# An early 64 KB store of zeros on the ScalarE DMA queue of a streaming p = 2 pooling kernel

## The chip, the cores and the metric

The kernel runs on one core of a Trainium2 chip. The metric is device time in microseconds of that core. Three runs of the kernel before gave 393.93, 393.96 and 393.99 us; the median is 393.96 us.

## What is computed

The input x is 32 x 256 x 4096 float32, the output 32 x 256 x 1024 float32. Each output is the root of the mean of the squares of four neighbours:

```python
for i in range(out_length):                   # out_length = 4096 // 4
    window = np.abs(x[:, :, 4*i:4*i+4]) ** p  # p = 2
    result[:, :, i] = np.mean(window, axis=-1) ** (1.0 / p)
```

The core reads 134.22 MB and writes 33.55 MB; nothing is read twice.

## The kernel before

Input and output are taken as flat arrays and cut into 20 pieces, numbered 0 to 19. A piece is 128 partitions by W = 13184 elements (52,736 bytes in each partition); piece 3 and the last one are a little narrower. Neighbouring pieces form six blocks (line 51), and within a block each partition holds one contiguous row of the flat array, so that a store of a block writes long rows.

Each piece goes through the same steps: a load by SyncE's queue (`load`, line 83); a square in place on ScalarE (`square`, line 89); two adds on VectorE that fold four squares into one sum (`pairs`, line 95, and `fours`, line 99); a square root with scale 1/4 on ScalarE (`roots`, line 102); and one store for each block (`store`, line 86). There are three input buffers `xt`, so load i + 3 is issued by SyncE after the adds of piece i. The results of a block gather in `ot`, four pieces wide. The sums of pieces 4, 8, 12 and 16 wait in `st`, in PSUM.

The order on each engine is written out by hand (`manual_schedule`, line 62): the three first loads at lines 122 and 123; a tiny square root at line 129, which brings in ScalarE's function table; the loop over pieces 0 to 16 from line 130; and a hand-written tail for pieces 17 to 19. The stores of blocks 0, 1 and 2 are issued by ScalarE on its own DMA queue (line 116, after the last roots of the block); the stores of blocks 3, 4 and 5 are issued by SyncE, on the queue that carries the loads. In the profile SyncE's queue is q1 and ScalarE's is q10. A DMA of 128 rows is seen in the trace as 128 packets, one for each row, eight on each of the 16 DMA engines, and 16 packets of 4 bytes that signal the end.

ScalarE's queue is used for the first time by the store of block 0.

Of the kernel before, what the change touches and what calls it, by code (L numbers as in the profile page):

```python
# [1 line left out]

# [4 lines left out]


@with_exitstack
def kernel(  # L10
    ctx: ExitStack,
    tc: tile.TileContext,
    x: bass.AP,
    p: float,
    kernel_size: int,
    out: bass.AP,
):

    nc = tc.nc

    assert float(p) == 2.0, "kernel specialized for p == 2"
    k = int(kernel_size)  # L30
    assert k == 4, "kernel specialized for kernel_size == 4"

    P = nc.NUM_PARTITIONS
    fp32 = mybir.dt.float32
    Act = mybir.ActivationFunctionType
    add = mybir.AluOpType.add
    xf = x.rearrange("b c l -> (b c l)")
    of = out.rearrange("b c l -> (b c l)")
    total = xf.shape[0] // P

    W = 13184
    R = W // k
    X_SLOTS = 3
    NARROW = W - 32
    LAST = total - 18 * W - NARROW
    widths = [W] * 3 + [NARROW] + [W] * 15 + [LAST]
    n = len(widths)
    assert 0 < LAST <= W and LAST % 16 == 0


    blocks = [[0, 1, 2, 3], [4, 5, 6, 7], [8, 9, 10, 11], [12, 13, 14, 15], [18, 16, 17], [19]]
    block_of = {i: b for b, group in enumerate(blocks) for i in group}
    block_width = [sum(widths[i] for i in group) for group in blocks]

    x_pool = ctx.enter_context(tc.tile_pool(name="x_pool", bufs=1))
    o_pool = ctx.enter_context(tc.tile_pool(name="o_pool", bufs=1))
    s_pool = ctx.enter_context(tc.tile_pool(name="s_pool", bufs=1, space=bass.MemoryType.PSUM))
    x_tiles = [x_pool.tile([P, W], fp32, name=f"xt{j}") for j in range(X_SLOTS)]
    o_tile = o_pool.tile([P, 4 * R], fp32, name="ot")
    first = o_pool.tile([P, 1], fp32, name="first")  # L60
    s_tile = s_pool.tile([P, 4096], fp32, name="st")
    ctx.enter_context(tc.manual_schedule())

    def rows(flat, b, div):
        at = sum(block_width[:b]) * P // div
        return flat[at:at + block_width[b] * P // div].rearrange("(p w) -> p w", p=P)


    free = x_tiles[17 % X_SLOTS]
    place = {i: o_tile[:, i % 4 * R:i % 4 * R + widths[i] // k] for i in range(16)}  # L70
    place[18] = free[:, R:2 * R]
    place[19] = free[:, 0:LAST // k]
    place[16] = free[:, 2 * R:3 * R]
    place[17] = free[:, 3 * R:4 * R]
    held = [o_tile[:, 0:w // k] for w in block_width[:4]] + [free[:, R:4 * R], place[19]]

    xs, loads, stores, sums, squares = {}, {}, {}, {}, {}

    def load(i):
        b = block_of[i]  # L80
        at = sum(widths[j] for j in blocks[b][:blocks[b].index(i)])
        xs[i] = x_tiles[i % X_SLOTS][:, 0:widths[i]]
        loads[i] = nc.sync.dma_start(out=xs[i], in_=rows(xf, b, 1)[:, at:at + widths[i]])  # L83

    def store(b, queue):
        stores[b] = queue.dma_start(out=rows(of, b, k), in_=held[b])  # L86

    def square(v):
        return nc.scalar.activation(out=v, in_=v, func=Act.Square)  # L89

    def pairs(v):

        q = v.rearrange("p (n j) -> p n j", j=k)
        h = v[:, 0:v.shape[1] // 2].rearrange("p (n j) -> p n j", j=2)
        return nc.vector.tensor_tensor(out=h, in0=q[:, :, 0:2], in1=q[:, :, 2:4], op=add)  # L95

    def fours(o, v):
        h = v[:, 0:v.shape[1] // 2].rearrange("p (n j) -> p n j", j=2)
        return nc.vector.tensor_tensor(out=o, in0=h[:, :, 0], in1=h[:, :, 1], op=add)  # L99

    def root(o, s):
        return nc.scalar.activation(out=o, in_=s, func=Act.Sqrt, scale=1.0 / k)  # L102

    summed = {i: s_tile[:, 0:R] if i in (4, 8, 12, 16) else place[i] for i in range(n)}

    def roots(*group):
        if len(group) == 1:
            root(place[group[0]], summed[group[0]])
        else:
            v = o_tile[:, group[0] % 4 * R:(group[-1] % 4 + 1) * R]  # L110
            r = root(v, v)
            if group[0] in (5, 9):

                implied(r, stores[block_of[group[0]] - 1])
        if group[-1] in (3, 7, 11):
            store(block_of[group[-1]], nc.scalar)

    def implied(later, earlier):

        tc.declare_no_dep(later.ins, earlier.ins, reason="implied by the other waits")  # L120

    for i in range(X_SLOTS):
        load(i)


    ahead = {4: (3,), 8: (7,), 12: (11,)}
    behind = {3: [(0, 1, 2)], 7: [(5, 6), (4,)], 11: [(9, 10), (8,)], 14: [(12,)], 15: [(13, 14)], 16: [(15,)]}

    root(first[:, :], nc.const_aps.tensor(1.0, (P, 1), fp32))
    for i in range(17):  # L130
        if i in ahead:
            roots(*ahead[i])
        s = square(xs[i])
        squares[i] = s
        if i == 3:
            implied(s, squares[0])
        if i in (3, 7, 11):

            for earlier in sums[i - X_SLOTS]:
                implied(s, earlier)  # L140
        for group in behind.get(i, []):
            roots(*group)
        sums[i] = pairs(xs[i]), fours(summed[i], xs[i])
        if i + X_SLOTS < n:
            load(i + X_SLOTS)

    store(3, nc.sync)
    square(xs[17])
    pairs(xs[17])
    fours(summed[17], xs[17])  # L150
    later = {18: 4608, 19: 2000}

    def shared_square(i):
        v = xs[i][:, 0:later[i]]
        nc.vector.tensor_tensor(out=v, in0=v, in1=v, op=mybir.AluOpType.mult)  # L155
        square(xs[i][:, later[i]:widths[i]])

    def shared_pairs(i):
        implied(pairs(xs[i]), loads[i])

    shared_square(18)
    roots(16)
    roots(17)
    shared_pairs(18)
    fours(summed[18], xs[18])
    shared_square(19)
    roots(18)
    store(4, nc.sync)
    shared_pairs(19)
    fours(summed[19], xs[19])  # L170
    roots(19)
    store(5, nc.sync)


# [1 line left out]
_INS = ['x', 'p', 'kernel_size']  # L176
_OUTS = [((32, 256, 1024), 'float32')]

_NUMBERS = {'p': 2.0, 'kernel_size': 4}


# [26 lines left out]
```

## Time and profile before

| what | value |
|---|---|
| median of three runs | 393.96 us |
| span of the profiled execution, first to last instruction | 392.3 us |
| median less span (what lies outside the span) | 1.7 us |
| ScalarE busy | 274.4 us, 70% |
| VectorE busy | 218.2 us, 56% |
| q1: share of the 16 DMA engines' span, packets | 87.4%, 3312 |
| q10: share of the 16 DMA engines' span, packets | 11.9%, 432 |
| moved over the span | 167.77 MB, 428 GB/s |
| issues by ScalarE's queue | 3, from 90.3 to 247.1 us |

The table gives no separate time for the profiled execution beyond its span: its own time is taken as the span and the 1.7 us around it, which together make the median. Busy times count compute instructions alone; a DMA's work is in the queue rows. In the table of 40 slices one slice is 9.8 us. In a table by stretches, a DMA packet is counted whole in the stretch in which it starts: over a few microseconds the share and the GB/s can be above what the engines can do, or far below it, and it is the product with the stretch's length that means something.

### The profile page before, as it was taken

Reading aid. Unit: us, or ns where it says so; the run is one execution under the profiler, and the core shown is the slowest. Engines: PE = TensorE matmul, PEld = TensorE weight load, DVE = VectorE, ACT = ScalarE, POOL = GpSimd, SP = SyncE. Lnnn points to the kernel's source line nnn. Section 1 sums busy time; section 2 is a strip of 40 time slices with the busy share of each in tenths; the row PEclk is TensorE's granted clock in tenths of the full one; section 3 lists DMA queues with packets and bytes.
Section 4 is the critical chain, followed back from the end, with each engine's and each line's share of the span. In section 5 each row is a group of like instructions: output and inputs, shape, how many; then the busy total and the mean of one; then the engine's idle time right before and its main releaser. Section 6 shows DMA issues by size and latency. Waiting matters only on the chain.

```text
span 392.3 us, 176 instructions
## 1 busy us (share of the span) xinstructions
DVE 218.2 (56%) x42; ACT 274.4 (70%) x37; POOL 0.2 (0%) x4
## 2 busy tenths in 40 slices
DVE  0009477580693274905942748069418485699970
ACT  1095695979950859799509597995098999969910
POOL 0000000000000000000000000000000000000000
DMA  8999999999999999999999999999999999999997
GB/s 344 430 430 430 430 440 435 452 457 366 430 430 430 430 430 430 430 441 446 452 446 441 436 430 436 430 430 430 430 430 430 430 430 430 430 453 415 430 413 342
DMA packets 3744, 167.77 MB, mean 428 GB/s; under 512 B 416, under 2 KB 416, under 8 KB 416
## 3 DMA queue, kind: packets, MB, share of 16 engines
q1 hardware_dynamic: 3312, 147.53, 87.4%
q10 hardware_dynamic: 432, 20.25, 11.9%
HBM read 134.22 MB, written 33.55 MB: 428 GB/s over the span
## 4 chain that ended last, share of the span: by engine, by line
DMA 43%; ACT 30%; DVE 23%; issue 0%; ACTq 0%; SPq 0%; DVEq 0%
DMA xt<-in_x_dram 43%; ACT xt L89 28%; DVE xt L95 14%; DVE ot L99 5%; DVE xt L99 3%; DVE xt L155 2%; ACT ot L102 2%; ACT xt L102 1%; ACTq L86 0%; SPq L83 0%; DVEq L95 0%
## 5 line engine op out<-in xcount | busy, mean ns | idle before, releaser
L89 ACT ACTIVATE xt<-xt 128x13184 f32<-128x13184 f32 (+3 forms) x20 | 216.7, 10847 | 92.3 <-DMA xt<-in_x_dram 91.0
L95 DVE TENSOR_TENSOR xt<-xt 128x6592 f32<-128x6592 f32 (+2 forms) x20 | 139.7, 6985 | 144.1 <-ACT xt L89 143.9
L99 DVE TENSOR_TENSOR ot<-xt 128x3296 f32<-128x3296 f32 (+1 forms) x13 | 46.7, 3592 | 17.9 <-DMA out_dram<-ot 17.6
L102 ACT ACTIVATE ot<-ot 128x6592 f32<-128x6592 f32 (+3 forms) x8 | 37.2, 4655 | 7.0 <-DVE ot L99 7.0
L102 ACT ACTIVATE xt<-xt 128x3296 f32<-128x3296 f32 (+1 forms) x3 | 8.5, 2836 | 8.8 <-DVE xt L99 8.8
L99 DVE TENSOR_TENSOR st<-xt 128x3296 f32<-128x3296 f32 x4 | 14.4, 3600 | 0.1
L99 DVE TENSOR_TENSOR xt<-xt 128x3296 f32<-128x3296 f32 (+1 forms) x3 | 10.4, 3461 | 0.1
L102 ACT ACTIVATE ot<-st 128x3296 f32<-128x3296 f32 x3 | 8.7, 2898 | 0.0
L155 DVE TENSOR_TENSOR xt<-xt 128x4608 f32<-128x4608 f32 (+1 forms) x2 | 7.2, 3593 | 0.0
L102 ACT ACTIVATE xt<-st 128x3296 f32<-128x3296 f32 x1 | 2.9, 2898 | 0.0
L102 ACT ACT_TABLE_LOAD x1 | 1.3, 1283 | 0.7 <-PEq L189 0.7
L102 ACT ACTIVATE first<-const-float32-1.0 128x1 f32<-128x1 f32 x1 | 0.2, 202 | 0.0
L189 POOL MEMSET const-bfloat16-1.0<- 128x1 bf16 x1 | 0.1, 101 | 0.0
L189 POOL MEMSET const-uint8-127<- 128x1 uint8 x1 | 0.1, 101 | 0.0
L189 POOL MEMSET const-float32-0.0<- 128x1 f32 x1 | 0.1, 98 | 0.2 <-issue 0.2
L189 POOL MEMSET const-float32-1.0<- 128x1 f32 x1 | 0.1, 98 | 0.0
## 6 DMA issues: line engine op xcount, KB each, us to landing
xt<-in_x_dram SPq DMA_DIRECT2D x18, 6592.0 KB, 29.8
out_dram<-ot ACTq DMA_DIRECT2D x2, 6592.0 KB, 35.1
out_dram<-ot SPq DMA_DIRECT2D x1, 6592.0 KB, 37.1
out_dram<-ot ACTq DMA_DIRECT2D x1, 6588.0 KB, 36.3
xt<-in_x_dram SPq DMA_DIRECT2D x1, 6576.0 KB, 24.7
xt<-in_x_dram SPq DMA_DIRECT2D x1, 5840.0 KB, 21.9
out_dram<-xt SPq DMA_DIRECT2D x1, 4944.0 KB, 16.1
out_dram<-xt SPq DMA_DIRECT2D x1, 1460.0 KB, 8.2
```

Of the source, the lines that this page charges most:

```text
L89: return nc.scalar.activation(out=v, in_=v, func=Act.Square)
L95: return nc.vector.tensor_tensor(out=h, in0=q[:, :, 0:2], in1=q[:, :, 2:4], op=add)
L99: return nc.vector.tensor_tensor(out=o, in0=h[:, :, 0], in1=h[:, :, 1], op=add)
L102: return nc.scalar.activation(out=o, in_=s, func=Act.Sqrt, scale=1.0 / k)
L155: nc.vector.tensor_tensor(out=v, in0=v, in1=v, op=mybir.AluOpType.mult)
L189: nc = _bacc.Bacc("TRN2", target_bir_lowering=False, num_devices=1)
```

## The change

A tile of zeros, 128 partitions by 128 elements (512 bytes in each), is added in SBUF. VectorE fills it ahead of everything else. After the three first loads have been issued by SyncE, ScalarE issues a DMA that stores it into the first 128 elements of each partition's row of output block 0. The proper store of block 0 overwrites these 64 KB later, and has to follow the store of zeros. Nothing is removed or reordered.

```diff
     s_tile = s_pool.tile([P, 4096], fp32, name="st")
+    zeros = o_pool.tile([P, 128], fp32, name="zeros")
     ctx.enter_context(tc.manual_schedule())
...
+    nc.vector.memset(zeros[:, :], 0.0)
     for i in range(X_SLOTS):
         load(i)
+    nc.scalar.dma_start(out=rows(of, 0, k)[:, 0:128], in_=zeros[:, :])
```

## The prediction

> **What bounds the kernel now.** I read the 40 slices first, then the chain of waits, then the DMA over short stretches.
>
> The two DMA rows of the slices:
>
> ```profile
> DMA  8999999999999999999999999999999999999997
> GB/s 344 430 430 430 430 440 435 452 457 366 430 430 430 430 430 430 430 441 446 452 446 441 436 430 436 430 430 430 430 430 430 430 430 430 430 453 415 430 413 342
> ```
>
> The DMA engines are at 90% or more in every slice but the first and the last; no compute engine is (70% and 56% in the table above). Slice 9 stands out with 366 GB/s, and it holds the first issue on ScalarE's queue, at 90.3 us.
>
> The chain of waits, by engine:
>
> ```profile
> DMA 43%; ACT 30%; DVE 23%; issue 0%; ACTq 0%; SPq 0%; DVEq 0%
> ```
>
> This seems to say that compute is half of the bound. It isn't: the chain steps back through squares and adds because a load waits for its buffer, but other transfers fill the engines meanwhile. In the trace's DMA packet records 16 packets are in progress at nearly every moment from 1.74 us (the first) to 390.5 us (the last ends at 390.91). So the time is the sum of packet times over 16 engines. A microsecond of DMA time saved anywhere comes off the end as long as compute keeps up; the tightest place is the last store: its issue ends at 383.5 us, its first packet starts at 386.8 us behind the store before it. Issue start to first packet was 1.0 us for the first load (0.73 to 1.74), so some 2.6 us are in hand (386.8 less 383.2 + 1.0).
>
> DMA over chosen stretches; columns: stretch in us, length, busy time of three engines, clock, DMA share, GB/s. A packet counts whole where it starts, so share times length is the mean packet time if each of the 16 engines starts one packet there:
>
> ```profile
> 1.00:4.00 3.00, 0.00 (x0) 1.21 (x2) 0.00 (x0) 1.00 0.89 281
> 4.00:6.00 2.00, 0.00 (x0) 0.00 (x0) 0.00 (x0) 1.00 0.97 422
> ...
> 91.50:94.50 3.00, 0.00 (x0) 3.00 (x1) 0.00 (x0) 1.00 0.96 281
> 94.50:96.50 2.00, 0.00 (x0) 2.00 (x1) 0.00 (x0) 1.00 0.98 422
> ...
> 170.50:172.40 1.90, 0.00 (x0) 1.90 (x1) 0.00 (x0) 1.00 1.02 444
> 248.00:250.00 2.00, 0.00 (x0) 2.00 (x1) 0.00 (x0) 1.00 0.98 422
> ```
>
> Each stretch holds 16 packets (281 GB/s x 3 us = 843 KB = 16 rows of 52.7 KB). A normal packet takes 1.95 us (0.97 x 2). Two sets don't: the very first (0.89 x 3 = 2.67 us) and those in flight when the first store of ScalarE's queue arrives (0.96 x 3 = 2.88 us). The packet records give the excess over 1.947 us as 0.72 us at the start and 0.94 us at 92 us. At the second and third store of that queue (issued at 169.3 and 247.1 us, last two rows) there is none: 1.02 x 1.9 = 1.94 and 0.98 x 2 = 1.96. So once in the run, all 16 engines lose about 0.94 us when ScalarE's queue is first used, all of it on the path that sets the end.
>
> **The change, part by part.**
>
> The fill on VectorE: the adds at line 99 write 3296 elements in 3.59 us, 1.09 ns each; 128 elements are 0.14 us, and the smallest fill of the page takes 0.10 us, so 0.1 to 0.25 us. VectorE is idle until 30.01 us: nothing.
>
> The new issue on ScalarE: 0.34 to 0.38 us by line 86's rows, and it waits for the fill. It starts at 0.73 + 0.1 to 0.25, about 0.9 us, and ends near 1.3 us. Behind it stand the table load (1.28 us) and the tiny root (0.20 us): done near 2.8 us instead of 2.2 us. ScalarE's first square waits for load 0 until 18.79 us, so that slack of 16 us hides it. SyncE's three issues at 0.73 to 2.06 us are on another sequencer; the new DMA is past none of them in its own queue, and its packets share the engines with theirs.
>
> The added wait: the proper store of block 0, issued at 90.31 us, must follow the store of zeros. Queued behind it on ScalarE is the square of piece 4 at 90.73 us. The zeros take turns with load 0's eight packets on each engine, so they land by about 18 us; the wait is over 70 us old. Nothing, or one instruction of 0.02 us (the semaphore rows of line 86) that the DMA's backlog hides.
>
> The packets: eight of 512 bytes on each engine, and a signal. The shortest rows of the trace are 11,680 bytes in 0.439 us and 52,736 bytes in 1.947 us: 0.0367 ns a byte and 10 ns a packet. By that line 512 bytes take 29 ns, eight 0.23 us, with the 9 ns of a signal 0.24 us. Bounds: nothing, if they fit in the start's idle time; above, a stall with each packet (a rival below). I take 0.24 us, which delays load 0 and all after it.
>
> The stall: 0.94 us should go at 92 us, if it belongs to the first use of the queue and a small store will do for it. What the same first use costs at the start the trace doesn't show. It comes about 0.2 us behind the first use of q1, whose own first packets lose 0.72 us. Bounds: nothing, if the two pass together; 0.94 us, if one follows the other. The nearest row is the start's 0.72 us, time in which the engines move little anyway: I let it hide 0.72 of the 0.94 us, so 0.22 us are still paid.
>
> What is late next: nothing new. The DMA stays the bound, and the 2.6 us at the last store shift with everything else.
>
> Sum against the profiled execution, 392.3 us of span and 1.7 us around it, which are the 393.96 us of the median: -0.94 + 0.22 + 0.24 = -0.48, so **393.48 us**.
>
> **The rivals.**
>
> *Full cover.* Both first uses pass together and the second costs nothing: -0.94 + 0.24 = -0.70, 393.26 us; with the zeros hidden as well -0.94, 393.02 us. For it: the issues lie 0.2 us apart. Against it: the stretched packets at 92 us started 1.6 to 2.0 us after the issue; by the same delay the stall would begin at 2.5 to 3 us, when data already flows. The Trainium skill ("HBM Reference", Latency) gives 0.2 us for an access on average and 2 us at high load; if the stall is such a latency it would be shorter at the start and this case would hold, but no run here shows it, and the start's 0.72 us speaks against a much shorter one.
>
> *Nothing saved, slower.* The stall follows q1's start-up in full, or it isn't the queue's first use that makes it but the first real store, so that it stays at 92 us. It decides if the engines handle one queue's first use after the other, or if 64 KB is too little to bring it on. Price: +0.24 us, 394.20 us. For it: the stall at 92 us held up another queue's packets, on all engines, so it isn't something that queues do side by side. Against: the stall coincides with the first packets of that queue, and start-up leaves room.
>
> *Small packets cost more.* If the engine waits for each small write, its eight turns hold up the loads: to lose the whole gain of 0.48 us, each turn needs 0.06 us beyond the 29 ns. At three times that, 0.18 us, the loss is 1.44 us and the result 393.48 + 1.44 = 394.92 us. Against: after a 4-byte signal of 9 ns the next packet starts 6 ns later in the records (98.789 and 98.795 us). The Trainium skill ("DMA: Bandwidth & Descriptors", Bandwidth) lists a 64 KB load from GpSimd at 0.95 us of DMA time and says that transfers below 64 KB are dominated by their descriptors; by that, as an estimate, the forecast's sum would be -0.94 + 0.22 + 0.95 = +0.23 us. That speaks against this change; no run here shows so small a transfer.
>
> *Paid twice.* The first use costs 0.94 us at the start, and the queue, idle from about 18 to 90 us, pays again. Against it: 45 us without issues between its own later stores (packets end at 124 and 202 us, the next issues come at 169 and 247 us) brought no second stall. 72 us is longer, so it isn't excluded: +0.94 + 0.24 = +1.18, 395.14 us.
>
> **How the numbers follow.** Forecast 0.51, full cover 0.17, nothing saved 0.24, small packets 0.04, paid twice 0.04. 0.2% of 393.96 us is 0.79 us, about what a measurement of this kernel can tell from no change. The forecast and the case of nothing saved are inside it. Full cover is beyond it (below 393.17 us) if the zeros are nearly free too or the stall was a little larger than its mean: 0.13 with what the forecast adds. Slower by more needs the stall twice or the dear packets: 0.08. The range goes from full cover with free zeros, 393.0 us, to nothing saved, 394.20 us, plus 0.1 us: 394.3 us. The forecast's own range is 393.2 to 393.75 us.
>
> **What would show it.** In the profile after: 16 packets at 92 us with 1.95 us instead of 2.88 us (the stall moved), slice 9 back near 430 GB/s, and first packets longer than 2.67 us by what the start still pays. Packets of 512 bytes at 29 ns each show the zeros' price; load 0 landing later than 18.77 us shows it with the stall's remainder. A stretch at 92 us that stays at 2.88 us would make the forecast wrong at its root, and so would ScalarE issuing the zeros much later than 1 us.

## The result

The changed kernel took 394.59 us (median of 20 runs, 394.38 to 394.77) against 394.01 us of the kernel before in the same session (20 runs, 393.88 to 394.24): ratio 1.0014, 95% interval 1.0009 to 1.002. It is slower by about 0.6 us, where -0.48 us was forecast, and it lies above the range, which ended at 394.3 us.

The profile after, a span of 392.7 us. The page's DMA rows, packet counts and queues:

```profile
DMA  8999999999999999999999999999999999999997
GB/s 345 435 430 430 430 434 429 440 457 387 430 430 430 430 430 440 440 440 435 435 435 446 440 435 435 430 430 430 430 430 430 430 430 430 430 462 405 430 440 313
DMA packets 3888, 167.84 MB, mean 427 GB/s; under 512 B 432, under 2 KB 560, under 8 KB 560
...
q1 hardware_dynamic: 3312, 147.53, 87.3%
q10 hardware_dynamic: 576, 20.31, 12.0%
```

The 128 packets of zeros are there (560 less 432), and slice 9, with the first proper store, is still the low one at 387 GB/s; a packet counts where it starts, so its distance to 430 isn't a measure of the loss. The stretches are; they have the same columns as those of before:

```profile
1.00:4.00 3.00, 0.00 (x0) 1.49 (x2) 0.00 (x0) 1.00 0.90 281
...
91.50:94.50 3.00, 0.00 (x0) 3.00 (x1) 0.00 (x0) 1.00 0.97 281
170.80:172.80 2.00, 0.00 (x0) 2.00 (x1) 0.00 (x0) 1.00 0.97 422
248.60:250.60 2.00, 0.00 (x0) 2.00 (x1) 0.00 (x0) 1.00 0.98 422
```

This decides it. The 16 packets in flight at 92 us take 0.97 x 3 = 2.91 us, before 2.88 us: the stall has not moved. By the packet records the excess over the normal 1.947 us is 0.97 us (0.94 before), and at the start 0.77 us (0.72 before). The second and third store have none, as before, and the chain of waits has the same shares (DMA 43%, ScalarE 30%, VectorE 23%).

The start, in order of time:

```profile
0.73 1.33 SPq L84 DMA_DIRECT2D xt<-in_x_dram  x3
0.82 0.17 DVE L123 MEMSET zeros<- 128x128 f32 x1 [0.82 <-PEq L192]
1.02 0.42 ACTq L126 DMA_DIRECT2D out_dram<-zeros  x1
1.47 1.28 ACT L103 ACT_TABLE_LOAD   x1 [1.47 <-DVE zeros L123]
2.76 0.20 ACT L103 ACTIVATE first<-const-float32-1.0 128x1 f32<-128x1 f32 x1
19.00 11.19 ACT L90 ACTIVATE xt<-xt 128x13184 f32<-128x13184 f32 x1 [16.03 <-DMA xt<-in_x_dram]
```

The fill, the issue and the tiny root stand where they were expected, and the first square starts 0.21 us later than before (19.00 against 18.79 us): that is the delay of load 0 by eight packets of zeros. In the records each takes 27 ns, so 0.22 us.

One number isn't in the profile. Each run has its time and its span. In 26 later runs of the kernel before, the time is 1.78 us longer than the span on average; in the 20 runs of the changed kernel 2.05 us. About 0.28 us more lie outside the span, where no row shows them.

### The profile page after: what moved, and what is told of

Same layout as the page of the kernel before. It is cut to its first block, busy times and chain, and to the rows that moved or that the text cites. A ratio compares the mean times of both kernels' runs of the same rounds, so it can differ in the third digit from the quotient of the medians.

```text
span 392.7 us, 179 instructions
## 1 busy us (share of the span) xinstructions
DVE 218.4 (56%) x43; ACT 274.4 (70%) x37; POOL 0.2 (0%) x4
## 4 chain that ended last, share of the span: by engine, by line
DMA 43%; ACT 30%; DVE 23%; issue 0%; ACTq 0%; SPq 0%; DVEq 0%
DMA xt<-in_x_dram 43%; ACT xt L90 28%; DVE xt L96 14%; DVE ot L100 5%; DVE xt L100 3%; DVE xt L158 2%; ACT ot L103 2%; ACT xt L103 1%; ACTq L87 0%; SPq L84 0%; DVEq L96 0%
```

## The experiments

**Which use of the queue stalls the engines.** Theory 1: the first full-size store. Theory 2: the queue's first use, and its use after a rest (the changed kernel has shown that first use alone isn't enough). Theory 3: the loads in flight at 92 us, not a store. Four kernels were run once each with a profile; the kernel before took 394.28 us beside them.

*zeros_late.* The store of zeros is issued between the squares of pieces 2 and 3:

```diff
-    nc.scalar.dma_start(out=rows(of, 0, k)[:, 0:128], in_=zeros[:, :])
...
+        if i == 3:
+            nc.scalar.dma_start(out=rows(of, 0, k)[:, 0:128], in_=zeros[:, :])
         s = square(xs[i])
```

> The changed kernel with the store of zeros issued later, just ahead of the square of piece 3 (about 61 us), so that ScalarE's queue rests some 29 us before the proper store at 90 us instead of 72 us. Theory 1 (the stall belongs to the first full-size store, whatever went before): packets in flight at 92 us stay at about 2.9 us. Theory 2 (a queue's first use stalls the engines, and so does its use after a long rest): the stall is at about 63 us, and packets at 92 us take 1.95 us. Theory 3 (the stall belongs to the loads in flight at that moment, not to a store): 2.9 us at 92 us, none at 63 us. Zeros cost 0.22 us in each case.

Measured: 394.75 us. ScalarE issued the zeros at 49.96 us, as soon as the square of piece 2 had begun, and their packets ran from 53.4 to 67.2 us, with no excess beside them. The queue then rested 23 us, and still the packets at 92 us had an excess of 0.97 us, as before:

```profile
92.00:94.60 2.60, 0.00 (x0) 2.60 (x1) 0.00 (x0) 1.00 1.12 325
```

That is 1.12 x 2.6 = 2.91 us. The queue's rests of about 45 us before the second and third store bring none. Theory 2 falls.

*no_store0.* The proper store of block 0 is left out (in the kernel before):

```diff
-            if group[0] in (5, 9):
+            if group[0] == 9:
...
-        if group[-1] in (3, 7, 11):
+        if group[-1] in (7, 11):
```

> The kernel before without the store of block 0, so that a part of the output is not written; the first use of ScalarE's queue is then the store of block 1. Theory 1 and theory 2: no stall at 92 us, and 0.9 to 1.0 us of it in the packets in flight 1.5 to 2 us after the issue of block 1's store. Theory 3: the stall stays with the loads at about 92 us (2.9 us packets) and none comes with the store of block 1. The time falls by about 6.75 MB at 430 GB/s, 15.7 us, if the DMA engines stay full.

Measured: 381.21 us. Stretches at 91 us and around the store of block 1, issued at 155.58 us:

```profile
91.50:93.50 2.00, 0.00 (x0) 2.00 (x1) 0.00 (x0) 1.00 0.98 422
...
157.20:160.20 3.00, 0.00 (x0) 3.00 (x1) 0.00 (x0) 1.00 1.09 281
```

Nothing at 92 us (0.98 x 2 = 1.96 us); at the new first store 1.09 x 3 = 3.27 us, an excess of 1.3 us. The stall goes with the store; theory 3 falls. The time fell by 13.1 us instead of 15.7 us: the DMA engines ran dry at 111.9 us until load 7, issued at 112.26 us, and its first packets had an excess of 0.63 us, much like those at the start.

*store0_sp.* The kernel before with block 0's store on the queue of the loads:

```diff
-            store(block_of[group[-1]], nc.scalar)
+            store(block_of[group[-1]], nc.sync if group[-1] == 3 else nc.scalar)
```

> The kernel before with the store of block 0 issued by SyncE on the queue of the loads; ScalarE's queue is first used by the store of block 1. Theory 1: a stall of 0.9 to 1.0 us when that store's first packets come up on q1, none at block 1's store. Theory 2: no stall with block 0's store, 0.9 to 1.0 us about 1.5 to 2 us after the issue of block 1's store. Theory 3: the stall stays with load 5's rows at about 92 us.

Measured: 394.36 us. This store waits its turn behind loads on q1 and its first packet starts at 112.2 us; the rows are the stretch just before it and the one before ScalarE's first store:

```profile
107.40:109.50 2.10, 2.07 (x2) 2.10 (x1) 0.00 (x0) 1.00 1.04 402
109.50:112.10 2.60, 2.60 (x1) 2.60 (x1) 0.00 (x0) 1.00 1.00 325
...
170.90:173.10 2.20, 0.00 (x0) 2.20 (x1) 0.00 (x0) 1.00 1.20 431
```

Together 0.91 us of excess ahead of the store by the records, on a queue that had carried seven loads. So it isn't the first use of ScalarE's queue. But theory 1 isn't the whole of it: ahead of ScalarE's first store, the second of the program, the packets had another 0.48 us (the last row holds 18 packets). Here two queues each paid at their first full-size store; in the kernel before, SyncE's first store, at 360 us, paid nothing.

*warm_full.* The early store as large as the proper one:

```diff
+    nc.vector.memset(o_tile[:, 0:block_width[0] // k], 0.0)
...
+    nc.scalar.dma_start(out=rows(of, 0, k), in_=o_tile[:, 0:block_width[0] // k])
```

> The changed kernel with the early store made as large as the proper one: the whole of block 0's rows, 52,704 bytes in each of 128 partitions, filled in the result tile itself. Theory 1: the stall comes with this store at about 15 to 20 us, and packets at 92 us take 1.95 us. Theory 2: the stall at the first use too, and possibly again after a rest of some 40 us. Theory 3: the loads at about 92 us or load 5's rows, wherever they are then, take 2.9 us. The time grows by about 15.6 us for the bytes, and by some us more where VectorE waits for the tile.

Measured: 419.31 us, 9.4 us more than the bytes explain: the engines lost step with one another and had scattered excesses to the end (8.5 us in all, against 2.0 us in the kernel before). Those are 6.5 us of the 9.4; neither they nor the rest are followed further here. For the question asked it is clear:

```profile
16.00:19.00 3.00, 0.00 (x0) 0.51 (x2) 0.00 (x0) 1.00 1.01 281
...
114.00:116.00 2.00, 0.00 (x0) 2.00 (x1) 0.00 (x0) 1.00 1.02 422
```

1.01 x 3 = 3.03 us ahead of the early store, an excess of 1.1 us. At the proper store, issued at 112.43 us, 0.1 us was left (1.02 x 2 = 2.04 us). A full-size early store does draw the stall to itself, and pays it in full.

**How large it must be.** *warm_8k* stores rows of 8 KB, *warm_16rows* 16 full-length rows (filled as in warm_full), *warm_512x16* as many bytes as warm_8k in pieces of 512 bytes.

```diff
+    nc.vector.memset(o_tile[:, 0:2048], 0.0)
...
+    nc.scalar.dma_start(out=rows(of, 0, k)[:, 0:2048], in_=o_tile[:, 0:2048])
```

> The changed kernel with rows of 8 KB instead of 512 bytes in the early store (1 MB, from the result tile). If a row's length brings on the stall, with a bound below 8 KB: excess of about 0.9 us in the packets in flight 1.5 to 2 us after its issue, and none at 92 us. If it takes longer rows or more bytes: the stall stays at 92 us. The bytes cost 1.0 MB at 430 GB/s, 2.4 us.

```diff
+    nc.scalar.dma_start(out=rows(of, 0, k)[0:16], in_=o_tile[0:16, 0:block_width[0] // k])
```

> The changed kernel with an early store of 16 full-length rows, 52,704 bytes each, from 16 partitions: one packet on each DMA engine, 0.84 MB, issued near 15 us. If the length of the packets brings on the stall: excess of about 0.9 us in flight at 16 to 17 us and none at 92 us. If it takes a volume of several MB: none at 16 us, the stall stays at 92 us. The bytes cost 1.95 us.

```diff
+    nc.vector.memset(o_tile[:, 0:16 * 136], 0.0)
...
+    nc.scalar.dma_start(
+        out=rows(of, 0, k)[:, 0:2048].rearrange("p (n j) -> p n j", j=128),
+        in_=o_tile[:, 0:16 * 136].rearrange("p (n j) -> p n j", j=136)[:, :, 0:128])
```

> The changed kernel with an early store of 1 MB in pieces of 512 bytes (16 for each partition, from a tile with gaps), as many bytes as the store of 8 KB rows, which brought the excess at 92 us down to 0.53 us. If the bytes written decide: about 0.5 us left at 92 us. If the length of a row decides: 0.95 us left at 92 us. The 2048 pieces, 128 on each engine, cost 128 x 27 ns = 3.5 us.

The stretch ahead of the proper store, warm_8k (issue at 93.24 us):

```profile
94.60:96.90 2.30, 0.00 (x0) 2.30 (x1) 0.00 (x0) 1.00 1.05 367
```

and warm_512x16 (issue at 101.32 us):

```profile
102.50:105.20 2.70, 0.00 (x0) 2.70 (x1) 0.00 (x0) 1.00 1.02 313
```

With 8 KB rows 1.05 x 2.3 = 2.42 us, 0.47 us of excess, 0.53 us with the packets after it; with the same megabyte in 512-byte pieces 2.75 us, 0.81 us of excess, 0.96 us with those after it. How far does this carry? Eleven profiles have the proper store and either no early store or the one of 64 KB; in them the excess there, counted in the same way, is 0.67 to 1.05 us (0.67 to 1.00 us in the five with the zeros, 0.84 to 1.05 us in the six without). So 0.53 us lies below all of them, but not by much, and one run of each kernel points to the length of the rows rather than the number of bytes without proving it. And warm_8k gained nothing: it had 0.34 us of new excess before 20 us, 0.25 us of it in loads at 18 us, while the early packets still ran, so about 0.87 us in all; its time of 396.96 us is the kernel before plus the bytes (eight packets of 0.309 us, 2.5 us) and 0.4 us outside the span. (warm_512x16 took 405.19 us: its store landed only at 54 us, VectorE waited for the tile, no load was in flight from 50.9 to 59.2 us, and the engines were empty from 53.8 us on.) warm_16rows, 407.55 us, tells little: all but one of the rows from 16 partitions alone took 2.5 to 5.7 us instead of 1.95, the engines lost step as in warm_full, and excesses of over 10 us spread through the run. The loads in flight at 16 to 19 us had 0.6 us of it, as did the packets between 96 and 106 us, around the first of the proper store.

**Queue or direction.** The load of piece 2 goes to ScalarE's queue, behind the square of piece 0:

```diff
-        loads[i] = nc.sync.dma_start(
+        loads[i] = (nc.scalar if i == 2 else nc.sync).dma_start(
...
-    for i in range(X_SLOTS):
+    for i in range(2):
         load(i)
...
+        if i == 0:
+            load(2)
```

> The kernel before with the load of piece 2 issued by ScalarE after the square of piece 0 (about 30 us), so that ScalarE's queue carries a full-size load before its first store. If the queue's first full-size use brings on the stall: excess near 32 us, none at 92 us. If it is the first full-size store, in that direction: none at 32 us, 0.85 to 1.0 us at 92 us as before. Time within 0.5 us of the kernel before in either case.

Measured: 400.37 us. ScalarE issued at 19.40 us, as soon as that square had begun, load 1 and load 2 shared the engines, and these then ran dry once (from 65.7 to 69.6 us, with 0.76 us of excess at the restart); the time is thus beyond what was expected. The stretches before the first packet of that load, and before the first packet of the first store:

```profile
22.00:24.00 2.00, 0.00 (x0) 2.00 (x1) 0.00 (x0) 1.00 0.98 422
...
95.55:98.50 2.95, 0.00 (x0) 2.95 (x1) 0.00 (x0) 1.00 1.00 286
```

0.98 x 2 = 1.96 us: a queue's first use by a full-size load costs nothing here. 1.00 x 2.95 = 2.95 us: the store on the same queue, now in use, pays 1.0 us. So in these runs, one of each kernel, it takes a store to bring on the stall, and a load of the same size doesn't.

**Where 0.6 us of loss come from.** The packets of zeros explain 0.22 us. For the rest the fill is varied. *memset_only* (and *memset_r5* with more runs) leaves out the store of zeros; *zeros_pool* (and *pool_r5*) fills on GpSimd:

```diff
-    nc.vector.memset(zeros[:, :], 0.0)
+    nc.gpsimd.memset(zeros[:, :], 0.0)
```

> The changed kernel with the fill of zeros but without its store. If the fill is free, as the prediction has it: the time of the kernel before within its spread (394.0 us), 1.7 to 1.8 us outside the span. If the fill brings the 0.3 us that the changed kernel has outside its span: 394.3 us and about 2.05 us outside the span. The stall at 92 us stays in both (first full-size store).

> The changed kernel with the zeros filled by GpSimd instead of VectorE. If the extra DMA makes the 0.3 us outside the span: as the changed kernel, 394.6 us, 2.05 us outside. If an added instruction on VectorE makes it: 394.3 us, 1.75 us outside.

> The changed kernel once more, beside the two that leave out one part each. Theory of two parts (0.28 us outside the span from the added VectorE instruction, 0.25 to 0.3 us of DMA time from the store of zeros): 0.5 to 0.6 us over the kernel before. Theory of one part (the store alone costs it, the 0.28 us outside is a matter of where the span begins): the same here; the next two tell it apart.

> The fill without the store, with enough runs for an interval. Two parts: 0.2 to 0.3 us over the kernel before. One part: no more than 0.1 us over it, though 0.28 us more lie outside the span.

> The store with the fill on GpSimd, with enough runs for an interval. Two parts: 0.25 to 0.3 us over the kernel before, about 0.28 us below the changed kernel. One part: as the changed kernel, 0.5 us over.

Beside 26 runs of the kernel before (394.07 us) on one chip (the last column is a mean):

| kernel | median us, runs | ratio, 95% interval | time less span, us |
|---|---|---|---|
| before | 394.07, 26 | | 1.78 |
| after_r5 (fill and store) | 394.42, 11 | 1.0012, 1.0003 to 1.0021 | 2.05 |
| memset_r5 (fill alone) | 394.22, 11 | 1.0004, 0.9995 to 1.0013 | 2.06 |
| pool_r5 (store, fill on GpSimd) | 394.24, 11 | 1.0006, 0.9996 to 1.0015 | 1.79 |

The medians add up, 0.15 + 0.17 = 0.32 against 0.35 us, but for either part by itself the interval holds 1, so neither is shown in the time. The 0.58 us of the first measurement didn't come again: the same kernel lost 0.35 us here, and about 0.2 us of the first loss stay unexplained. In an earlier session memset_only was at 394.22 us (1.0006, 0.9996 to 1.0015) and zeros_pool at 394.37 us (1.0008, 0.9998 to 1.0017) against 394.09 us. What no spread blurs is the last column: every run of these kernels with a fill on VectorE has 2.0 us or more outside its span, every run of the others 1.73 to 1.83 us, with or without the store of zeros. Part of it only shifts: memset_r5's span is 0.13 us shorter than that of the kernel before (mean 392.16 against 392.29 us), which leaves 0.15 us. By the medians, then, the fill would cost about half of what lies outside, which neither of the two pure theories has; the interval leaves that open.

Is it the fill, its place, or any instruction on VectorE? *memset_late* has the fill ahead of piece 17's adds, *tt_early* a one-element add at the start instead, *memset_two* two half fills; none of them stores the zeros. The added lines of the three, in this order:

```diff
     store(3, nc.sync)
+    nc.vector.memset(zeros[:, :], 0.0)
...
+    one = nc.const_aps.tensor(1.0, (P, 1), fp32)
+    nc.vector.tensor_tensor(out=zeros[:, 0:1], in0=one, in1=one, op=add)
...
+    nc.vector.memset(zeros[:, 0:64], 0.0)
+    nc.vector.memset(zeros[:, 64:128], 0.0)
```

> The kernel before with the fill of the zeros tile on VectorE late, ahead of piece 17's adds, and no store of it. If any fill on VectorE, wherever it stands, brings the 0.28 us outside the span: 2.05 us outside. If only an instruction that VectorE runs at the start does: 1.78 us outside. The span is that of the kernel before.

> The kernel before with a tiny add on VectorE at the start (one element for each partition) in place of the fill, and no store. If any early instruction on VectorE brings the 0.28 us outside the span: 2.05 us outside. If it is the fill as an operation: 1.78 us outside.

> Two fills on VectorE, each of half the tile, and no store. If each instruction added to VectorE brings 0.28 us outside the span: 2.3 us outside. If it is a step that the first one takes: 2.05 us, as with one.

Outside the span lay 2.06, 2.05 and 2.19 us. A fill at the start, a fill near the end and a one-element add each brought the same 0.28 us, so neither the place nor the operation decides; the second fill brought another 0.13 us. A count of VectorE's instruction records in the traces, semaphore waits included, puts all the kernels in order: 52 (no_store0) and 53 records go with 1.78 us in the profiled execution, 54 with 2.05 to 2.06 us, and 55 with 2.17 to 2.19 us. The kernels with 55 are memset_two and the four whose early store comes from the result tile: these have one fill alone, but also one more wait on VectorE, for that store. That a wait counts like a fill was not varied by itself. The times of these single runs were 394.21, 394.24 and 394.55 us, where the kernel before had 394.38 us beside the first two and a median of 394.07 us beside the third: too few to put a time on it. What happens in those 0.28 us no trace here shows.

## Why the prediction was wrong, step by step

*What bounds the kernel:* right. The DMA engines stay full in the profile after, and what the zeros cost load 0 arrives at the end: in pool_r5, which has the store but no fill on VectorE, the mean span is 0.20 us longer than in the kernel before.

*The issue, the table load, the wait:* right. The issue is at 1.02 us (0.9 forecast), the tiny root done at 2.96 us (2.8), and the wait is one semaphore instruction of 0.02 us on ScalarE.

*The packets:* right, 0.22 us for 0.24. They take turns one for one with rows of 52.7 KB, so that the 64 KB land 19.9 us after their issue, at 20.9 us (about 18 us was forecast), but cost the engines only their own time. The Trainium skill ("DMA: Bandwidth & Descriptors", Bandwidth) lists 0.95 us of DMA time for a load of 64 KB issued from GpSimd; for this store, issued by ScalarE beside a stream of loads, the measurement is a quarter of that, and it decides here.

*The stall:* here the prediction failed: "0.94 us should go at 92 us, if it belongs to the first use of the queue and a small store will do for it". Neither half holds. It comes with the first store of long rows, also on a queue that loads have used; rows of 512 bytes leave it where it was (0.97 us), full rows move it and pay in full (1.1 us), and with rows of 8 KB one run had 0.53 us left and 0.34 us earlier. This isn't a complete rule: store0_sp had a second stall of 0.48 us. The trace of before couldn't tell this from first use: the first store was both at once. The step went from "first on this queue" to "because of this queue"; a store and a load differ in direction as well, and a row of 512 bytes differs a hundredfold in length. The cover of 0.72 us at the start was therefore never tested.

*The fill:* "nothing" was wrong. Within the span it costs nothing. Outside it 0.28 us appear; of these about 0.15 us remain in the time by the medians, which the interval doesn't separate from none.

*The rivals:* "nothing saved" was the mechanism that held, in its second form (the first real store makes the stall, so that it stays at 92 us), with 394.20 us. Add 0.15 us for the instruction on VectorE and it stands at 394.35 us; 394.42 us were measured in the later session, and 394.59 us in the first, with the 0.2 us that stay unexplained. A stall paid twice, small packets that cost more and full cover did not happen. The range ended too low in part because the sum had no term outside the span.

The Trainium skill ("HBM Reference", Latency) has 0.2 us on average and 2 us at high load for an access. That the stall would shrink in a quiet moment remains open: in warm_full it came at 16 us, with loads on all engines, and had 1.1 us.

## What stays open

Why the first long-row store holds up all 16 engines for 0.7 to 1.3 us (0.67 in after_r5, 1.3 in no_store0) isn't settled. It is as large as a restart of emptied engines (0.63 to 0.76 us here) or larger, but they were not empty, and store0_sp had a second one of 0.48 us on another queue. How the rows' length between 512 bytes and 52.7 KB sets it was seen at one size only, 8 KB, in one run. An early store that moves useful bytes instead of zeros wasn't tried.

## What to carry to other kernels

A stall that comes once can go with any of the things that are new at that moment: the queue, the direction, the size. Change one of them alone in a cheap kernel before paying to "warm up" another. In a kernel that fills its DMA engines, a warm-up gains only if its bytes take less time than it saves; here the early store that drew the whole stall to itself also paid it, and one that runs while the engines are idle wasn't tried. And when tenths of a microsecond matter, look at the time outside the span too: one instruction added to VectorE's program showed up there and in no row of the profile but its own.

## What was not expected of the hardware

- The first store with long rows cost 0.7 to 1.3 us on all engines, on ScalarE's queue as on SyncE's (0.91 us in store0_sp); a full-size load as first use of a queue cost nothing.
- One instruction more on VectorE brought 0.28 us outside the span (1.78 to 2.06 us), a second one 0.13 us more (2.19 us), one on GpSimd none (1.79 us).
- Engines that run dry lose more than the gap: the first packets after a gap of 1.3 us (no_store0), 3.9 us (load2_act) and 5.4 us (warm_512x16) took 0.63, 0.76 and 0.71 us longer.
- Packets of 512 bytes between rows of 52.7 KB took 27 ns each, without a visible pause.
